# Seven block products in three of eight pairs, and two pairs with adding DMA, in the recurrent-value and gate groups

## The chip, the cores and the metric

The kernel runs on one core of a Trainium2 chip. The metric is the device time of one execution in microseconds. The engines are called by the profile's names: PE is TensorE (PEld its weight loads), DVE is VectorE, ACT is ScalarE, POOL is GpSimd, and SP is the engine that issues most DMAs.

## The reference

The kernel computes one residual block of a streaming encoder on x of 256 tokens and 2048 features, all in float32: an input projection to 7168 columns, eight heads of chunked attention, eight heads of a gated linear recurrence (HGRN2), an output projection, a SwiGLU layer of width 5632 and a last norm.

```python
h = rmsnorm(x, norm1_gain)
proj = h @ w_in          # q_a k_a v_a | q_r f_r i_r g_r, 1024 columns each
attn = rmsnorm(chunk_band_attention(q_a, k_a, v_a, rel_bias), attn_out_gain)
rec = hgrn2_mixer(q_r, f_r, i_r, g_r, lb, grn_norm_gain)   # gated by silu(g_r)
x = x + concat(attn, rec) @ w_out
h2 = rmsnorm(x, norm2_gain)
x = x + (silu(h2 @ w_gate) * (h2 @ w_up)) @ w_down
return rmsnorm(x, final_gain)
```

The change concerns two column blocks of the input projection: i_r, the recurrent values (block "i0" in the code), and g_r, the gates (block "g0"), 1024 columns each.

## The kernel before

**Precision.** Each float32 operand is split in two parts of a shorter format: a high part (ACT copies it with rounding, L89) and a low part (DVE subtracts the high part from the value, L90). A product of two matrices is then three matmuls: high by high, high by low, low by high (L331 to L338, line 336). Weights come from memory in chunks of 1 MB (128 partitions x 2048 columns, that is four blocks of 512 columns) and are split on the core. The input and its split stay in `hx`.

**Groups and pairs.** A `Group` (L315) computes a result of 256 tokens x 1024 columns as four blocks c00, c01, c10, c11 of 128 x 512, each in a bank of accumulators. It walks over the 2048 inputs in eight pairs of 128 rows; a pair needs one chunk of weights. An item of the group's list is a kind and a pair number. Kind "d" (full) makes eight block products, 24 matmuls. Kind "s" makes seven, by a scheme of Strassen's sort: 21 matmuls, some into further banks (m1, m5, m6, m7) that `spread` adds into the output tiles after the last such pair. For it DVE forms differences of weight blocks (`ta`, `tb`, L383 to L387), splits them too, and needs sums of the input blocks, four per pair, that `row_sums` (L290) makes ahead of time. Kind "a" makes eight products like "d", but the low part of the weights comes without DVE: ACT writes the negated high part into a tile (`lower`, L352) and a DMA issued by POOL adds the weights to it from memory (L356). Before the change only the later stages (output projection and gate-up) have "a" items; their chunk lies in a tile of its own, `rawa`, and the adding DMA moves 512 KB.

**The order of the input stage.** Values of attention, then keys and queries of attention, the forget gates f0 and f1 and recurrent queries r0 and r1 of the first four recurrent heads, the recurrent values (one group for all eight heads, `vals`, L874), f2, f3, r2, r3, the gates (`gates`, L885), and then the output projection. `Natural` (L817) is the class of both groups that change. Its items are d0 d1 d2 s6 d3 s7 d4 d5. The row sums for pairs 6 and 7 are in `wsa`, made during attention (`x_sums`, L678); `xs_of` (L814) reads them. In the gates, `wsa` is written anew after item 6, with sums for the output projection (L851).

**Small work between.** What belongs to attention and to the recurrence stands in a list of closures, `queue`. `tick` (L111) runs one entry, or two when more than eight wait, after every chunk of a transposed block (L155). A `Natural` group runs as many entries after an item as its `ticks` say (L848).

**Preparing one item ahead.** `run_groups` (L450) traces an item's matmuls and then the preparation of the next item. When the item after that is an "a", `prepare` traces `begin` (its load) and `lower` first: `lower(0)` ahead of the other splits, and `lower(1)` ahead of them too if the item at hand is an "s", else behind them. The low copies are pinned behind what was traced last on ACT (`keep_in_program_order`, L355); other instructions are ordered when the program is built, by a planner with a list of priorities and estimated durations, and each engine then executes its own list in order.

**Buffers.** Chunks rotate through three places (`wraw`), split halves through four places for high and four for low parts (`wsp`: an "s" takes four of each, a "d" two), differences through one place each (`ta`, `tb` in `dn`). A tile can be written when the last reader of its place is done. SP issues the loads in a fixed order, each behind the one traced before (`dma`, L82).

**Attention's tiles.** For each head `att_scores` (L494) fills `s` (384 columns), `att_probs` (L514) transposes it and fills `pT` (128 columns) and `px` (2 x 256), and `att_values` (L523) multiplies by the values. Three heads are in work at a time: a queue entry runs the values of head n-2, the probabilities of head n-1 and the scores of head n. Each of the three tiles has two places.

Of the kernel before, what the change touches and what calls it, by code (L numbers as in the profile page):

```python
# [8 lines left out]
F32 = mybir.dt.float32  # L9
F32R = mybir.dt.float32r  # L10
I32 = mybir.dt.int32
AF = mybir.ActivationFunctionType
ALU = mybir.AluOpType
# [3 lines left out]
P = 128  # L17
S = 256
# [3 lines left out]
W = 512  # L22
# [23 lines left out]
def hybrid_block(ctx: ExitStack, tc: tile.TileContext, x, xT, w_in, w_out, w_gu, w_down,  # L46
                 bias, gains, lbnd, fgain, out):
    nc = tc.nc
# [33 lines left out]
    def dma(o, i):  # L82
        with ExitStack() as st:
            if prev:
                st.enter_context(tc.issue_after(prev[-1]))
            prev.append(nc.sync.dma_start(o, i).ins)

    def split(hi, lo, src):
        nc.scalar.activation(hi, src, AF.Copy)  # L89
        nc.vector.tensor_tensor(lo, src, hi.bitcast(F32), ALU.subtract)  # L90
# [18 lines left out]
    queue = []  # L109
# [7 lines left out]
    def drain():  # L117
        while queue:
            queue.pop(0)()
# [46 lines left out]
    wsa = tc.tile_pool(name="wsa", bufs=1)  # L166
    own = {"wsa": wsa.__enter__().tile([P, 2, 4, 2, P], F32R, name="wsa")}
    mix = tc.tile_pool(name="mix", bufs=1)
    mixp = mix.__enter__()
    ab = tc.tile_pool(name="ab", bufs=1)  # L170
    abp = ab.__enter__()
# [4 lines left out]
    hx = act_t.tile([P, KD, 2, S], F32R, tag="hx", name="hx")  # L176
# [113 lines left out]
    def row_sums(dst, hi, lo, in_order=False):  # L290
        n = hi.shape[1] // 2
        a = dn.tile([P, 2, 2, S], F32, tag="ta", name="a")[:, 0:n]
        sm = dn.tile([P, 4, 2, P], F32, tag="tb", name="sm")[:, :, 0:n]
        first = nc.vector.tensor_tensor(a, hi.rearrange("p (j k) t -> p j k t", k=2).bitcast(F32),
                                        lo.rearrange("p (j k) t -> p j k t", k=2).bitcast(F32), ALU.add)
        if in_order:
            tc.keep_in_program_order(first)
        a11, a12, a21, a22 = a[:, :, 0, 0:P], a[:, :, 1, 0:P], a[:, :, 0, P:S], a[:, :, 1, P:S]
        nc.vector.tensor_tensor(sm[:, 0], a21, a22, ALU.add)
        nc.vector.tensor_tensor(sm[:, 1], sm[:, 0], a11, ALU.subtract)  # L300
        nc.vector.tensor_tensor(sm[:, 2], a11, a21, ALU.subtract)
        nc.vector.tensor_tensor(sm[:, 3], a12, sm[:, 1], ALU.subtract)
        split(dst[:, 0], dst[:, 1], sm)
# [11 lines left out]
    class Group:  # L315
# [25 lines left out]
            return load_chunk(self.src, self.base + j).rearrange("p (b n) -> p b n", n=W)  # L341

        def begin(self, j):
            raw = own["low"].tile([P, 4, W], F32, name="rawa")
            flat, src = raw.rearrange("p b n -> p (b n)"), self.src[self.base + j]
            if self.src is w_out:
                tc.keep_in_program_order(nc.gpsimd.dma_start(out=flat, in_=src))
            else:
                dma(flat, src)
            self.begun = j, raw, []  # L350

        def lower(self, k):  # L352
            j, raw, low = self.begun
            wl = own["low"].tile([P, 2, W], F32R, tag="low", name="low", bufs=3)
            tc.keep_in_program_order(nc.scalar.activation(wl, raw[:, 2 * k:2 * k + 2], AF.Copy, scale=-1.0))  # L355
            nc.gpsimd.dma_start(out=wl.rearrange("p b n -> p (b n)"),  # L356
                                in_=self.src[self.base + j, :, 2 * k * W:2 * (k + 1) * W], accum_op=ALU.add)
            low.append(wl)

        def prepare_begun(self, j):  # L360
            (_, raw, low), self.begun = self.begun, None
            tiles = []
            for k in range(2):
                wh = wsp.tile([P, 2 * W], F32R, tag="wh", name="wh")
                nc.scalar.activation(wh, raw[:, 2 * k:2 * k + 2].rearrange("p b n -> p (b n)"), AF.Copy)
                tiles.append([(wh[:, i * W:(i + 1) * W], low[k][:, i]) for i in range(2)])
            return [(f"c{t}{h}", self.lhs(2 * j + k, t), tiles[k][h if k == 0 else 1 - h], terms)
                    for terms in ((0, 2), (1,)) for k in range(2) for t in range(NT) for h in range(2)]

# [124 lines left out]
    def att_scores(box, hd, kq, qx, g):  # L494
        h = hd % 4
        sc = paux.tile([P, 384], F32, tag="aux", name="sc")
        nc.tensor.matmul(sc[:, 0:128], lhsT=kq[:, 1, h, :], rhs=kq[:, 0, h, :], start=True, stop=True)  # L497
        kh, kl, qh, ql = kx[:, g, 0, h, :], kx[:, g, 1, h, :], qx[:, 0, h, :], qx[:, 1, h, :]
        nc.tensor.matmul(sc[:, 128:384], lhsT=qh, rhs=kh, start=True, stop=False)
        nc.tensor.matmul(sc[:, 128:384], lhsT=qh, rhs=kl, start=False, stop=False)  # L500
        nc.tensor.matmul(sc[:, 128:384], lhsT=ql, rhs=kh, start=False, stop=True)
        s = box["s"] = abp.tile([P, 384], F32, tag="s", name="s", bufs=2)
        nc.vector.scalar_tensor_tensor(s, sc, ASCALE, G[:, hd, :], ALU.mult, ALU.add)
        nm_ = small.tile([P, 2], F32, tag="nmax", name="nmax")
        sm = small.tile([P, 2], F32, tag="asum", name="asum")
        for t, (a, b) in enumerate(halves):
            nc.vector.tensor_reduce(nm_[:, t:t + 1], s[:, a:b], AX.X, ALU.max, negate=True)
            nc.scalar.activation(s[:, a:b], s[:, a:b], AF.Exp, bias=nm_[:, t:t + 1],
                                 accum_out=sm[:, t:t + 1])
        nc.vector.reciprocal(sm, sm)  # L510
        for t, (a, b) in enumerate(halves):
            nc.vector.tensor_scalar(s[:, a:b], s[:, a:b], sm[:, t:t + 1], None, ALU.mult)

    def att_probs(box):  # L514
        pp = paux.tile([P, 384], F32, tag="aux", name="pp")
        for j in range(3):
            nc.tensor.transpose(pp[:, j * P:(j + 1) * P], box["s"][:, j * P:(j + 1) * P], ident)  # L517
        pT = box["pT"] = abp.tile([P, P], F32, tag="pT", name="pT", bufs=2)
        px = box["px"] = abp.tile([P, 2, S], F32R, tag="px", name="px", bufs=2)
        split(px[:, 0, :], px[:, 1, :], pp[:, 0:256])  # L520
        nc.vector.tensor_copy(pT, pp[:, 256:384])

    def att_values(box, hd, vx, v1, at):  # L523
        h = hd % 4
        hc = slice(h * P, (h + 1) * P)
        px = box["px"]
        po = paux.tile([P, S], F32, tag="aux", name="po")
        nc.tensor.matmul(po, lhsT=vx[:, 0, hc], rhs=px[:, 0, :], start=True, stop=False)
        nc.tensor.matmul(po, lhsT=vx[:, 0, hc], rhs=px[:, 1, :], start=False, stop=False)
        nc.tensor.matmul(po, lhsT=vx[:, 1, hc], rhs=px[:, 0, :], start=False, stop=False)  # L530
        nc.tensor.matmul(po[:, P:S], lhsT=v1[:, hc], rhs=box["pT"], start=False, stop=True)
        nc.scalar.copy(at[:, h, :], po)
# [42 lines left out]
    def attention_end():  # L575
        def flush(n):
            def run():
                att_values(*ago[n - 2])
                if n - 1 < 8:
                    att_probs(ago[n - 1][0])  # L580
            return run
        queue.append(flush(8))
        queue.append(flush(9))
        queue.append(lambda: att_square(1))
        queue.append(att_rstd)
        for g in range(2):
            for i in range(2):
                queue.append(lambda g=g, i=i: att_norm(g, i))
# [87 lines left out]
    vxs = [abp.tile([P, 2, W], F32R, tag="t4", name="vx", bufs=NT4) for _ in range(2)]  # L676
    v1s = [abp.tile([P, W], F32, tag="ht", name="v1", bufs=3) for _ in range(2)]
    def x_sums(j):  # L678
        ks = slice(12 + 2 * j, 14 + 2 * j)
        row_sums(own["wsa"][:, :, :, j:j + 1, :], hx[:, ks, 0, :], hx[:, ks, 1, :])  # L680

    run_groups([Values(0, [("d", j) for j in range(KQ)], w_in, 0, x_pair, None)])
    for g in range(2):
# [15 lines left out]
        if g == 1:  # L699
            queue.insert(0, lambda: att_square(0))  # L700
            dma(lbr.rearrange("p r h -> p (r h)"), lbnd)
            lower_bound()
    attention_end()


    def hgrn_gate(st, g, i):
# [105 lines left out]
        split_scaled(mr[:, 0, ks, tok], mr[:, 1, ks, tok], pt, gg)  # L812

    def xs_of(j, i):  # L814
        return own["wsa"][:, 0, i, j - 6, :], own["wsa"][:, 1, i, j - 6, :]

    class Natural(Group):  # L817
        hold, ready = 1, None

        def __init__(self, nm, func, name, ticks):  # L820
            items = [(c, int(j)) for c, j in zip("dddsdsdd", "01263745")]
            super().__init__(0, items, w_in, chunk_of(nm), x_pair, xs_of)
            self.func, self.ticks = func, ticks
            self.out = [t4([P, NT, W], name) for _ in range(2)]
# [54 lines left out]
    hgrn_front(1)  # L879
    queue.extend(lambda t=t: hgrn_o(sts[1], t) for t in range(NT))  # L880
    x2 = res.tile([P, NT, D], F32, tag="res", name="x2")
    mr = mixp.tile([P, 2, 8, S], F32R, tag="mr", name="mr")
    for t in range(NT):
        dma(x2[:, t, :], x[t])
    gates = Natural("g0", AF.Silu, "gn", {0: 2, 1: 2, 2: 1, 6: 2})  # L885
    for g in range(2):
        sts[g]["gn"] = gates.out[g]

# [59 lines left out]
            Out(1, [(c, int(j)) for c, j in zip("asdsassd", "20316457")], w_out, 8, o_of, wsum_of)]  # L948

    run_groups([gates], wout[0])  # L950
    drain()
    for g in range(2):
        for t in range(NT):
# [274 lines left out]
```

## Time and profile before

| What | Value |
|---|---|
| Median of 3 runs | 1131.99 us (1131.68 to 1132.94) |
| Time of the profiled execution | 1131.58 us |
| Its span, first to last instruction | 1129.9 us |
| Mean granted clock of TensorE | 0.998 |
| Instructions | 14399 |
| Read from memory | 245.92 MB |

The page shows one execution. The lines that matter are the busy time of each engine, the chain of waits that ended last (which engine sets the end), and the groups of instructions with their mean duration. Time of the profile runs from the start of the span. The group of recurrent values lies at about 197 to 240 us, the gates at 291 to 333 us, and the output projection follows.

### The profile page before, as it was taken

The numbers are of one execution on the slowest core, as the hardware profiler recorded it, in microseconds if no ns is written. First come the engines' busy times: TensorE is split into PE (matmuls) and PEld (weight loads), VectorE is DVE, ScalarE is ACT, GpSimd is POOL, SyncE is SP. The second block draws the span as 40 slices with busy tenths as digits, with TensorE's granted clock in tenths as the row PEclk, the third lists the DMA queues.
The fourth block names the chain that finished last, engine by engine and source line by source line (L and its number), as shares of the span: only waits on it lengthen the run. The fifth ranks groups of instructions, "written<-read, shape, count | busy, mean of one in ns | idle before, by whom it ended". The sixth has DMA issues, their size and how long they took to land.

```text
span 1129.9 us, 14399 instructions
## 1 busy us (share of the span) xinstructions
PE 1120.4 (99%) x5344; PEld 936.8 (83%) x5344; DVE 990.0 (88%) x1294; ACT 725.3 (64%) x931; POOL 45.9 (4%) x73
## 2 busy tenths in 40 slices
PE   9999999999999999999999999999999999999997
PEld 7888888888888888888888888888888888888885
DVE  7867778996999998789889989989989999899986
ACT  7555656575966666676676676776766565555563
POOL 0000000000000000000000010010010000000000
PEclk9999999999999999999999999999999999999999
DMA  8665544656355768778788878778788756655652
GB/s 335 211 215 190 182 154 149 224 187 259 140 198 183 227 198 324 223 223 228 264 256 236 267 246 248 266 239 253 254 244 249 286 194 219 223 186 187 222 190 108
DMA packets 40246, 251.05 MB, mean 222 GB/s; under 512 B 4592, under 2 KB 5104, under 8 KB 13424
## 3 DMA queue, kind: packets, MB, share of 16 engines
q1 hardware_dynamic: 32832, 220.51, 53.1%
q0 software_dynamic: 7200, 29.36, 13.4%
q8 instruction: 42, 0.69, 0.2%
q10 hardware_dynamic: 144, 0.26, 0.1%
q14 instruction: 28, 0.23, 0.1%
HBM read 245.92 MB, written 4.19 MB: 221 GB/s over the span
## 4 chain that ended last, share of the span: by engine, by line
PE 98%; DVE 1%; ACT 0%; issue 0%; POOL 0%; ACTq 0%; POOLq 0%
PE c L336 62%; PE m L336 16%; PE acc L151 10%; PE acc L153 5%; PE ptr L281 1%; DVE wl L90 0%; PE wm L181 0%; PE po L792 0%; PE pa L765 0%; PE pp L517 0%; ACT wh L89 0%; PE po L794 0%; PE pc L772 0%; PE pa L780 0%; PE sc L497 0%
## 5 line engine op out<-in xcount | busy, mean ns | idle before, releaser
L90 DVE TENSOR_TENSOR wl<-raw,wh 128x1024 fp32r<-128x1024 f32 (+1 forms) x368 | 403.1, 1112 | 60.8 <-ACT wh L89 58.8
L89 ACT ACTIVATE wh<-raw 128x1024 fp32r<-128x1024 f32 (+1 forms) x368 | 351.8, 971 | 157.5 <-PE c L336 78.6
L336 PE MATMUL c<-wh,h 128*128 128x512 f32 x928 | 274.2, 390 | 0.0
L336 PEld LDWEIGHTS c<-wh,h 128*128 128x128 f32 x928 | 174.1, 188 | 36.6 <-DVE ff L1010 0.3
L151 PE MATMUL acc<-hx,wh 128*128 128x512 f32 x512 | 180.0, 395 | 0.0
L153 PE MATMUL acc<-hx,wl 128*128 128x256 f32 x512 | 143.2, 280 | 0.0
L89 ACT ACTIVATE wh<-ta 128x1024 fp32r<-128x1024 f32 x66 | 70.1, 1062 | 88.5 <-PE c L336 44.2
L336 PE MATMUL c<-wl,h 128*128 128x512 f32 x304 | 119.4, 393 | 0.0
L89 ACT ACTIVATE wh<-tb 128x1024 fp32r<-128x1024 f32 x66 | 70.1, 1062 | 69.0 <-PE c L336 36.3
L151 PEld LDWEIGHTS acc<-hx,wh 128*128 128x128 f32 x512 | 96.0, 188 | 21.4
L336 PE MATMUL c<-wh,hx 128*128 128x512 f32 x336 | 105.8, 393 | 0.0
L90 DVE TENSOR_TENSOR wl<-ta,wh 128x1024 fp32r<-128x1024 f32 x66 | 80.7, 1222 | 19.0 <-ACT wh L89 19.0
L153 PEld LDWEIGHTS acc<-hx,wl 128*128 128x128 f32 x512 | 96.5, 189 | 0.1
L90 DVE TENSOR_TENSOR wl<-tb,wh 128x1024 fp32r<-128x1024 f32 x66 | 80.6, 1221 | 12.2 <-ACT wh L89 9.8
L336 PE MATMUL c<-wh,fh 128*128 128x512 f32 x224 | 87.3, 390 | 0.2 <-DVE ff L1002 0.2
L336 PE MATMUL c<-wh,fl 128*128 128x512 f32 x224 | 87.2, 389 | 0.0
L336 PE MATMUL c<-wl,fh 128*128 128x512 f32 x224 | 87.2, 389 | 0.0
L336 PE MATMUL m<-wh,hs 128*128 128x512 f32 x240 | 81.9, 389 | 0.0
L385 DVE TENSOR_TENSOR ta<-raw 128x1024 f32<-128x1024 f32 x66 | 80.6, 1221 | 0.9
L336 PEld LDWEIGHTS c<-wh,hx 128*128 128x128 f32 x336 | 63.3, 189 | 13.7 <-ACT wh L89 0.5
L336 PEld LDWEIGHTS c<-wl,h 128*128 128x128 f32 x304 | 57.1, 188 | 14.1 <-DVE wl L90 2.5
L336 PE MATMUL c<-wl,hx 128*128 128x512 f32 x168 | 65.2, 393 | 0.0
(354 smaller groups left out, 1735.6 us busy)
## 6 DMA issues: line engine op xcount, KB each, us to landing
raw<-in_w_gu_dram SPq DMA_DIRECT2D x68, 1024.0 KB, 7.0
raw<-in_w_in_dram SPq DMA_DIRECT2D x54, 1024.0 KB, 4.8
raw<-in_w_down_dram SPq DMA_DIRECT2D x44, 1024.0 KB, 4.8
rawa<-in_w_gu_dram SPq DMA_DIRECT2D x20, 1024.0 KB, 6.3
low<-in_w_gu_dram POOLq DMA_DIRECT2D x40, 512.0 KB, 6.9
raw<-in_w_out_dram SPq DMA_DIRECT2D x14, 1024.0 KB, 4.9
x<-in_x_dram SPq DMA_DIRECT2D x2, 1024.0 KB, 7.9
rawa<-in_w_out_dram POOLq DMA_DIRECT2D x2, 1024.0 KB, 7.0
```

The lines of the kernel that those rows point to most:

```text
L89: nc.scalar.activation(hi, src, AF.Copy)
L90: nc.vector.tensor_tensor(lo, src, hi.bitcast(F32), ALU.subtract)
L151: nc.tensor.matmul(ps[m].rearrange("p j t -> p (j t)"), lhsT=wh[:, col], rhs=both, start=kt == 0, stop=False)
L153: nc.tensor.matmul(ps[m][:, 0, :], lhsT=wl[:, col], rhs=rhs[:, kt, 0, :], start=False, stop=kt == KD - 1)
L281: nc.tensor.transpose(pt[:, j, t, :], nat(t)[:, n0 + j * P:n0 + (j + 1) * P], ident)
L336: nc.tensor.matmul(self.bank[n], lhsT=a, rhs=b, start=self.left[n] == self.total[n], stop=self.left[n] == 1)
L385: nc.vector.tensor_tensor(ta, raw[:, 1:3], raw[:, 0:2], ALU.subtract)
```

## The change

- The items of a `Natural` group become d0 a1 s6 d2 s7 s5 a3 d4: three full pairs, three by seven products, two with adding DMA.
- Pair 5 needs row sums. `x_sums(-1)` makes them, as a queue entry behind attention's last, into a new tile `x5`. It takes the place `mr`, which attention's keys `kx` had before and the recurrence's output `mr` has afterwards; `mr` itself is therefore asked for after the gates.
- For this stage an "a" item loads its chunk through the three rotating places (no `rawa`), and makes its low part in four tiles of one block each, with a negating copy of 512 columns and an adding DMA of 256 KB per tile.
- To make room for these, attention's tiles share four places of 512 columns, tag `bx`: `s` and `pT` of a head are one tile, `px` another, and the low tiles use the same four places.
- The gates run three queue entries after item 1 and none after item 2 (before: two and one).

```diff
         def begin(self, j):
+            if self.src is w_in:
+                self.begun = j, self.load(j), []
+                return
...
         def lower(self, k):
             j, raw, low = self.begun
+            if self.src is w_in:
+                low.append([])
+                for b in range(2 * k, 2 * k + 2):
+                    wl = abp.tile([P, W], F32R, tag="bx", name="low", bufs=4)
+                    tc.keep_in_program_order(nc.scalar.activation(wl, raw[:, b], AF.Copy, scale=-1.0))
+                    nc.gpsimd.dma_start(out=wl, in_=self.src[self.base + j, :, b * W:(b + 1) * W], accum_op=ALU.add)
+                    low[k].append(wl)
+                return
...
-            low.append(wl)
+            low.append([wl[:, i] for i in range(2)])
...
-        s = box["s"] = abp.tile([P, 384], F32, tag="s", name="s", bufs=2)
+        bx = box["bx"] = abp.tile([P, W], F32, tag="bx", name="bx", bufs=4)
+        s = box["s"] = bx[:, 0:384]
...
-        pT = box["pT"] = abp.tile([P, P], F32, tag="pT", name="pT", bufs=2)
-        px = box["px"] = abp.tile([P, 2, S], F32R, tag="px", name="px", bufs=2)
+        pT = box["pT"] = box["bx"][:, 384:W]
+        px = box["px"] = abp.tile([P, 2, S], F32R, tag="bx", name="px", bufs=4)
...
     def x_sums(j):
+        if j < 0:
+            own["x5"] = mixp.tile([P, 2, 4, 1, P], F32R, tag="mr", name="x5")
         ks = slice(12 + 2 * j, 14 + 2 * j)
-        row_sums(own["wsa"][:, :, :, j:j + 1, :], hx[:, ks, 0, :], hx[:, ks, 1, :])
+        row_sums(own["wsa"][:, :, :, j:j + 1, :] if j >= 0 else own["x5"], hx[:, ks, 0, :], hx[:, ks, 1, :])
...
     attention_end()
+    queue.append(lambda: x_sums(-1))
...
-            items = [(c, int(j)) for c, j in zip("dddsdsdd", "01263745")]
+            items = [(c, int(j)) for c, j in zip("dasdssad", "01627534")]
...
-    mr = mixp.tile([P, 2, 8, S], F32R, tag="mr", name="mr")
...
-    gates = Natural("g0", AF.Silu, "gn", {0: 2, 1: 2, 2: 1, 6: 2})
+    gates = Natural("g0", AF.Silu, "gn", {0: 2, 1: 3, 6: 2})
...
     run_groups([gates], wout[0])
+    mr = mixp.tile([P, 2, 8, S], F32R, tag="mr", name="mr")
     drain()
```

More of the change, by code (lines that the diff above doesn't have):

```diff
@@ L365, in prepare_begun @@
                 nc.scalar.activation(wh, raw[:, 2 * k:2 * k + 2].rearrange("p b n -> p (b n)"), AF.Copy)
-                tiles.append([(wh[:, i * W:(i + 1) * W], low[k][:, i]) for i in range(2)])
+                tiles.append([(wh[:, i * W:(i + 1) * W], low[k][i]) for i in range(2)])
             return [(f"c{t}{h}", self.lhs(2 * j + k, t), tiles[k][h if k == 0 else 1 - h], terms)
@@ L814, in xs_of @@
     def xs_of(j, i):
+        if j == 5:
+            return own["x5"][:, 0, i, 0, :], own["x5"][:, 1, i, 0, :]
         return own["wsa"][:, 0, i, j - 6, :], own["wsa"][:, 1, i, j - 6, :]
```

## The prediction

> **What bounds the kernel now.** I read the page first (engines, then the chain that ended last), then the chain in order of time, then the busy time by stage for the two groups that the change touches, then their instructions one by one.
>
> ```profile
> span 1129.9 us, 14399 instructions
> PE 1120.4 (99%) x5344; PEld 936.8 (83%) x5344; DVE 990.0 (88%) x1294; ACT 725.3 (64%) x931; POOL 45.9 (4%) x73
> PE 98%; DVE 1%; ACT 0%; issue 0%; POOL 0%; ACTq 0%; POOLq 0%
> ```
>
> The last line is the chain: 98% of the span is TensorE (PE) handing to itself. Matmul ends are modelled, so "99% busy" alone would not do; the starts decide. The chain in order of time (start, length, what, count) shows their spacing in the stretch of values (before 239.6), at the start of the gates, and at the few places where it widens:
>
> ```profile
> 197.57 16.35 PE c L336 x72
> 290.90 16.34 PE c L336 x72
> 319.48 2.29 PE m L336 x9
> 353.90 0.73 PE c L336 x2
> 354.63 0.89 PE m L336 x3
> 368.01 2.14 PE c L336 x8
> ```
>
> 72 matmuls of 512 columns in 16.35 us are 0.227 us each, and the two stretches agree. At that spacing the last four rows would take 2.04, 0.45, 0.68 and 1.82 us, so they hold stalls of 0.25, 0.28, 0.21 and 0.32 us. PE is the bound, with about 1 us of stalls from the gates to the output projection. A change moves the end by the matmuls that it removes plus the stalls that it adds or takes away.
>
> The two groups by stage (PE, PEld, VectorE = DVE, ScalarE = ACT, POOL busy, granted clock, DMA share, GB/s), with the stretch ahead of the first, and below them the rows for the product line L336 alone:
>
> ```profile
> 190.00:200.00 10.00, 10.00 (x56) 8.61 (x55) 9.98 (x18) 7.86 (x12) 0.00 (x0) 1.00 0.47 152
> 197.40:239.60 42.20, 42.20 (x189) 34.92 (x188) 39.20 (x46) 28.52 (x33) 0.00 (x0) 1.00 0.58 202
> 290.70:333.00 42.30, 42.30 (x188) 34.73 (x188) 41.48 (x56) 31.11 (x40) 0.00 (x0) 1.00 0.50 176
> 197.40:239.60 42.20, 42.19 (x186) 34.73 (x186) 1.00 0.58 202
> 290.70:333.00 42.30, 42.30 (x186) 34.69 (x186) 1.00 0.50 176
> ```
>
> In the gates DVE is busy 41.48 of 42.30 us: PE sets the pace, with DVE hardly behind it. ACT has 11 us free there, POOL is idle, DMA is half idle.
>
> **The matmuls.** A full pair costs 8 products of 3 matmuls, 24; a pair by seven products 21. Before, six full and two seven: 6x24 + 2x21 = 186, the count in the rows. After, three full, two with adding DMA (also 24) and three seven: 5x24 + 3x21 = 183. Twice three at 0.227 us: **-1.36 us**. This gain is certain as long as PE is fed. The Trainium skill (TensorE: Matmul & The Clock Gate, Back-to-back issue gap) gives about 131 ns as the sustained spacing at 512 columns and 216 ns for an isolated gap; by the first the term would be -0.79 us, but the rows here show 227 ns, near the second, and the measurement decides.
>
> **DVE and ACT work.** Durations by form in the gates, with the sums of pair 7's size on hx, and the low copies and adding DMAs of the later stages (for those: min/median/max ns; landing in us; the last two rows give size and median landing):
>
> ```profile
> L90 DVE TENSOR_TENSOR wl<-raw,wh 128x1024 fp32r<-128x1024 f32 x14 | 16.9, 1216 | 0.0
> L90 DVE TENSOR_TENSOR wl<-raw,wh 128x512 fp32r<-128x512 f32 x2 | 1.4, 684 | 0.0
> L385 DVE TENSOR_TENSOR ta<-raw 128x1024 f32<-128x1024 f32 x2 | 2.4, 1208 | 0.0
> L387 DVE TENSOR_TENSOR tb<-raw,tb 128x512 f32<-128x512 f32 x2 | 1.4, 688 | 0.0
> L89 ACT ACTIVATE wh<-raw 128x1024 fp32r<-128x1024 f32 x13 | 13.5, 1056 | 4.6 <-PE c L336 2.9 <-DVE wl L90 1.7
> L89 ACT ACTIVATE wh<-raw 128x512 fp32r<-128x512 f32 x2 | 1.3, 626 | 0.3 <-PE m L336 0.3
> L294 DVE TENSOR_TENSOR a<-hx x2: 685/688/692, 36.3 to 39.4; 128x512 f32<-128x512 f32 x2
> L302 DVE TENSOR_TENSOR sm<-a,sm x12: 283/416/424, 39.0 to 1059.2; 128x256 f32<-128x256 f32 x7, 128x128 f32<-128x128 f32 x5
> L356 POOL DMA_DIRECT2D low<-in_w_gu_dram x40: 860/866/892, 458.8 to 861.9; - x40
> DMA to landing us min/median/max: 5.3/7.0/12.7
> low<-in_w_out_dram POOLq DMA_DIRECT2D x4, 512.0 KB, 10.1
> raw<-in_w_in_dram SPq DMA_DIRECT2D x54, 1024.0 KB, 4.8
> ```
>
> On DVE a full pair is 2x1.22 = 2.43 us; a seven-product pair is 0.68 + 1.22 (its blocks), 1.21 + 2x0.69 (differences), 2x1.22 (their splits), 6.92; an adding pair nothing. Per group 6x2.43 + 2x6.92 = 28.4 becomes 3x2.43 + 3x6.92 = 28.1: -0.38. On ACT a full pair is 2.11, a seven-product pair 3.80, an adding pair 2.11 + 4x0.63 = 4.62; per group 20.3 becomes 27.0, +6.7, inside the free 13.7 and 11.2 us. So no engine gets more than it can do; what can cost is the order.
>
> **The row sums of pair 5** (L690, L718): 0.69, four of about 0.28 and a split of 0.68, 2.5 us of DVE once. Counted out, the queue runs them in r1's second chunk: one entry more makes it longer than eight, so it pops two once more and the normalising entries come a chunk earlier. DVE is full there (9.98 of 10), but pair 1's 2.43 us leave just then. Net 0; without that cover at most 2.5 us once.
>
> **Pair 5 behind pair 7, the costly spot.** Two seven-product pairs now follow each other with the low copies of pair 3 between them on ACT: the first is pinned behind what was traced last on ACT, pair 7's fourth split. The same split in the gates before (start, length in us; the first row is r3's evacuation ahead of the gates, the last two low copies of a gate-up group):
>
> ```profile
> 288.84 0.69 ACT L161 COPY tb<-acc 128x256 f32<-128x256 f32 x2
> ...
> 317.28 0.39 PE L336 MATMUL m<-wh,hx 128*128 128x512 f32 x1
> 317.57 1.07 ACT L89 ACTIVATE wh<-tb 128x1024 fp32r<-128x1024 f32 x1 [0.68 <-DVE tb L387]
> 318.62 1.23 DVE L294 TENSOR_TENSOR a<-ma 128x1024 f32<-128x1024 f32 x1
> 319.77 1.22 DVE L90 TENSOR_TENSOR wl<-tb,wh 128x1024 fp32r<-128x1024 f32 x1
> 321.04 0.19 PEld L336 LDWEIGHTS m<-wl,wsa 128*128 128x128 f32 x1 [0.40 <-DVE wl L90]
> ...
> 524.37 2.00 ACT L355 ACTIVATE low<-rawa 128x1024 fp32r<-128x1024 f32 x2
> ```
>
> Pair 7 starts on PE at 317.28. Its fourth tile takes over the place of the pair before, free only then; 15 matmuls later, 3.4 us, it is needed, and ACT 1.07 plus DVE 1.22 leave 1.1 us. One other DVE instruction of 1.23 us (L294) stood between, and PE waited. After the change, counted from pair 7's start: its fourth ACT split ends at 1.4 and four low copies, 0.53 us apart, at 3.5 (two of 1024 columns take 2.00 together in the last row, so each overlaps the one before by 0.1, and 0.63 - 0.1 = 0.53). Pair 5's first split follows until 4.0 and DVE's until 4.7, needed at 4.99 (21 matmuls and one). Its second: ACT 5.0, DVE 6.2, needed at 5.67 (25 matmuls): 0.55 us late. The third and fourth have more room. Bounds per group: nothing, if the low copies find a gap or pair 5's copies are issued ahead of them, to 0.55; I take the middle, **+0.55 us for both groups**.
>
> **What costs nothing.** Pair 1's adding DMAs in the gates: four low copies after r3's evacuation end near 292.0 (289.5 + 4x0.63), and POOL issues at 0.87 us each, the last near 292.8. Its tile is needed 20 matmuls into pair 1, at 290.9 + 24x0.227 + 4.5 = 300.9: 8.1 us for a landing with a median of 7.0 for twice the bytes. The 4 MB more (16 pieces of 256 KB) are small beside DMA half idle. Pair 5's chunk takes the place of the chunk of pair 2, two pairs ahead instead of three, since pair 3's is loaded first. I estimate that pair 2 is split by its own start on PE, 24 + 21 matmuls or 10.2 us before pair 5, against 4.8 us for a load.
>
> Attention's tiles: the place of head n is free after the values of head n, which PE issues ahead of the scores of head n+2; so no new wait. mr takes its place after pair 5's sums are read, and is first written after the gates. The mixed keys move one item earlier, the same three copies.
>
> **The sum.** The profiled execution took 1131.58 us, 1.68 around its span; -1.36 + 0.55 = -0.81 gives 1130.77. Against the median of the three runs, 1131.99 (0.41 above the profiled one): **1131.2**.
>
> **Rivals.**
> *Slower: pair 1's low tiles land late.* The place is the first adding pair of each group, where the copies can't start before the recurrent queries leave PE. For it: the four adding transfers of the output projection took 10.1 us. Against it: those were of 512 KB, and the gate-up ones took 7.0. At 10.1 the last lands 2.0 us late in each group: -1.36 + 4.0 = +2.6, 1134.6. It decides from 8.1 us; at 8.8 it eats the whole gain, at 9.9 it passes 0.2%.
> *Faster: later stalls go as well.* With DVE 0.38 us lighter per group and nothing of pair 3 to split, the 0.25 and the 0.28 + 0.21 + 0.32 us of stalls may vanish: -1.36 - 1.06 = -2.42, 1129.6. Against it: those sit where attention, gates and output projection crowd DVE, and that work stays.
> *No gain in matmuls: DVE is the bound.* Then the end follows DVE: -2x0.38 + 2.5 = +1.74, 1133.7, and the change does not do what it says. For it: 41.48 of 42.30 in the gates; against it: 72 matmuls at 0.227 on both sides, and DVE free for 3 us in the values. The Trainium skill (Perfetto Trace Analysis, Identifying the Most-Contended Engine) wants TensorE judged by its weight loads rather than by matmul occupancy; that is 83% here, below DVE's 88%, and would make this the likeliest case. The even spacing of starts in the trace speaks against it.
>
> **Numbers.** Forecast 0.68 (its own 1130.6 to 1131.7 by the bounds of pair 5's stall), late low tiles 0.14, later stalls gone 0.10, DVE the bound 0.08. The range takes in the second and third rival and the milder half of the first: 1129.6 to 1133.7. A measurement of this kernel can tell about 0.2%, 2.3 us, from no change. Faster by more: most of the second rival, 0.08. Slower by more: the graver part of the first and what I can't see, 0.14. Within: 0.78.
>
> **What would show it.** Right: 183 products in L336's rows for either group; the groups about 0.7 us shorter, less any stall; a small wait of PE at pair 5's second product for DVE or ACT, none at pair 1's low products; the row sums on hx three times, the third ahead of the values; spacing still 0.227. Wrong: PE waiting for a low tile, stalls of over 1 us in a group, or a stretch outside the two groups that grows or shrinks by more than half a microsecond.

## The result and the profile after

The changed kernel takes **1151.05 us** (median of 5 runs, 1148.76 to 1152.89) against 1131.99 us (1131.68 to 1133.19): ratio 1.0167, 95% interval 1.0155 to 1.0178. It is slower by 19 us, where 1131.2 us was forecast. The profiled execution took 1151.12 us, its span 1149.1 us, 19.2 above the span before.

The page of the changed kernel, the lines that answer to those of before:

```profile
span 1149.1 us, 14463 instructions
...
PE 1125.9 (98%) x5338; PEld 938.5 (82%) x5338; DVE 992.9 (86%) x1302; ACT 737.7 (64%) x953; POOL 59.4 (5%) x89
...
q0 software_dynamic: 9504, 33.56, 15.4%
...
PE 91%; DMA 4%; DVE 3%; ACT 1%; issue 0%; SPq 0%; ACTq 0%
PE c L336 58%; PE m L336 15%; PE acc L151 9%; PE acc L153 5%; DMA low<-in_w_in_dram 4%; PE ptr L281 1%; DVE wl L90 1%; ACT wh L89 1%; DMA raw<-in_w_in_dram 0%; PE pa L780 0%; PE po L807 0%; DVE at L565 0%; PE pp L529 0%; DVE ma L90 0%; ACT low L361 0%
...
low<-in_w_in_dram POOLq DMA_DIRECT2D x16, 256.0 KB, 7.2
```

PE has six matmuls fewer, as counted, and still "98% busy": that share hides the loss, because a modelled end stretches over a wait. The chain shows it: PE fell from 98% to 91%, and the new entry is the adding DMA into the low tiles, 4%. The 4%, 46 us of the span, isn't what was lost: the chain follows a transfer back to its issue, also through time in which PE still worked. What PE lost is in the view of its waits (who waited <- for whom: us in total, times, longest):

```profile
PE c L336 <- DMA low<-in_w_in_dram: 13.4, 5, 3.9
PE wm L181 <- POOL ew L182: 1.1, 1, 1.1
```

Five waits, 13.4 us, where before there was none at a transfer. The issues of the adding pieces, on POOL's timeline (start, length, what, count, and in brackets how long POOL had idled, and for whom):

```profile
199.14 2.79 POOL L362 DMA_DIRECT2D low<-in_w_in_dram  x3 [88.03 <-DVE tb L162]
203.94 0.88 POOL L362 DMA_DIRECT2D low<-in_w_in_dram  x1 [2.01 <-ACT qd L772]
228.64 2.60 POOL L362 DMA_DIRECT2D low<-in_w_in_dram  x3 [23.82 <-ACT low L361]
232.52 0.87 POOL L362 DMA_DIRECT2D low<-in_w_in_dram  x1 [1.28 <-ACT wh L89]
300.71 2.62 POOL L362 DMA_DIRECT2D low<-in_w_in_dram  x3 [67.32 <-PE po L809]
304.73 0.87 POOL L362 DMA_DIRECT2D low<-in_w_in_dram  x1 [1.41 <-DMA low<-in_w_in_dram]
330.87 2.62 POOL L362 DMA_DIRECT2D low<-in_w_in_dram  x3 [25.26 <-PE c L336]
335.43 0.86 POOL L362 DMA_DIRECT2D low<-in_w_in_dram  x1 [1.95 <-ACT wh L89]
```

The same picture four times: three pieces go out together, and the fourth 1.3 to 2.0 us after POOL could have issued it. The releasers named differ from row to row and none has to do with this transfer; only one row names an earlier piece of the same kind. By the landings in the trace the first of each three had landed 0.26 to 0.32 us before the fourth went out (at 203.68 the one issued at 199.14). So the fourth looks held until the first has landed; experiment 7 tests it. Now the end of each first adding pair, in the chain in order of time (values, then gates):

```profile
198.27 1.58 ACT low L361 x3
199.84 12.98 DMA low<-in_w_in_dram x2
212.83 0.04 issue
212.87 2.07 PE c L336 x4
214.95 1.28 PE m L336 x3
216.23 2.22 PE c L336 x6
...
300.52 4.21 PE c L336 x19
304.73 9.61 DMA low<-in_w_in_dram
314.34 0.04 issue
314.39 2.07 PE c L336 x4
316.46 1.28 PE m L336 x3
317.74 2.56 PE c L336 x6
```

The fourth piece of the gates, issued at 304.73, lands at 314.34, and PE goes on 0.04 us later. Then the spacing is wrong too: 13 matmuls take 5.57 us in the values and 5.91 in the gates, where 13 x 0.227 is 2.95. The stretches say why (PE, PEld, DVE, ACT, POOL busy, granted clock, DMA share, GB/s):

```profile
207.00:211.00 4.00, 0.96 (x3) 0.49 (x3) 3.49 (x4) 0.77 (x1) 0.00 (x0) 1.00 1.07 270
211.00:215.00 4.00, 2.13 (x5) 1.74 (x6) 0.29 (x1) 0.00 (x0) 0.00 (x0) 0.51 0.47 193
215.00:219.00 4.00, 4.00 (x13) 3.10 (x13) 1.23 (x1) 1.57 (x2) 0.00 (x0) 0.64 0.00 0
309.00:314.00 5.00, 1.51 (x7) 0.93 (x5) 4.59 (x7) 4.97 (x6) 0.00 (x0) 0.95 1.01 251
314.00:319.00 5.00, 4.61 (x11) 3.65 (x12) 2.89 (x4) 1.96 (x3) 0.00 (x0) 0.50 0.26 107
```

Ahead of the end of the wait the DMA engines are busy throughout (a share of 1.07 in the first row and 1.01 in the fourth). Behind it PE runs at about half the clock for some 5 us in the values and 6 in the gates: 2.6 us lost in the values, 3.0 in the gates.

The account: 13.4 us of waits + 5.6 of slow clock - 1.36 of products = 17.6; with 0.8 at pair 5 (below) 18.4 of the 19.2. Nothing lies outside the two groups: by the starts of their products, first to last, the values take 51.6 us instead of 42.0, the gates 51.9 instead of 42.3, 19.2 in sum.

### The profile page after: what moved, and what is told of

The parts are those of the page before. It is cut to its first block, busy times and chain, and to the rows that moved or that the text cites. A ratio compares the mean times of both kernels' runs of the same rounds, so it can differ in the third digit from the quotient of the medians.

```text
span 1149.1 us, 14463 instructions
## 1 busy us (share of the span) xinstructions
PE 1125.9 (98%) x5338; PEld 938.5 (82%) x5338; DVE 992.9 (86%) x1302; ACT 737.7 (64%) x953; POOL 59.4 (5%) x89
## 3 DMA queue, kind: packets, MB, share of 16 engines
q0 software_dynamic: 9504, 33.56, 15.4%
## 4 chain that ended last, share of the span: by engine, by line
PE 91%; DMA 4%; DVE 3%; ACT 1%; issue 0%; SPq 0%; ACTq 0%
PE c L336 58%; PE m L336 15%; PE acc L151 9%; PE acc L153 5%; DMA low<-in_w_in_dram 4%; PE ptr L281 1%; DVE wl L90 1%; ACT wh L89 1%; DMA raw<-in_w_in_dram 0%; PE pa L780 0%; PE po L807 0%; DVE at L565 0%; PE pp L529 0%; DVE ma L90 0%; ACT low L361 0%
## 5 line engine op out<-in xcount | busy, mean ns | idle before, releaser
L90 DVE TENSOR_TENSOR wl<-raw,wh 128x1024 fp32r<-128x1024 f32 (+1 forms) x360 | 393.4, 1109 | 68.8 <-ACT wh L89 66.7
L89 ACT ACTIVATE wh<-raw 128x1024 fp32r<-128x1024 f32 (+1 forms) x360 | 342.3, 967 | 168.0 <-PE c L336 80.8
L90 DVE TENSOR_TENSOR wl<-ta,wh 128x1024 fp32r<-128x1024 f32 x68 | 83.2, 1223 | 19.8 <-ACT wh L89 19.7
L336 PE MATMUL c<-wh,hx 128*128 128x512 f32 x312 | 95.0, 395 | 0.2 <-ACT wh L89 0.2
L90 DVE TENSOR_TENSOR wl<-tb,wh 128x1024 fp32r<-128x1024 f32 x68 | 83.1, 1222 | 10.6 <-ACT wh L89 8.2
L396 DVE TENSOR_TENSOR ta<-raw 128x1024 f32<-128x1024 f32 x68 | 83.1, 1223 | 3.8 <-DMA raw<-in_w_in_dram 1.7
L336 PEld LDWEIGHTS c<-wh,hx 128*128 128x128 f32 x312 | 59.1, 190 | 13.3 <-ACT wh L89 0.9
L367 POOL DMA_DIRECT2D low<-in_w_gu_dram x40 | 34.4, 859 | 393.9 <-ACT low L366 258.8
```

The costliest lines, as they stand in the source:

```text
L336: nc.tensor.matmul(self.bank[n], lhsT=a, rhs=b, start=self.left[n] == self.total[n], stop=self.left[n] == 1)
L367: nc.gpsimd.dma_start(out=wl.rearrange("p b n -> p (b n)"), in_=self.src[self.base + j, :, 2 * k * W:2 * (k + 1) * W], accum_op=ALU.add)
L396: nc.vector.tensor_tensor(ta, raw[:, 1:3], raw[:, 0:2], ALU.subtract)
```

## Experiments

The theory after this look: the low tiles of both adding pairs are late, because their copies are made late, adding pieces are slow, and the fourth is held. The rivals: the new order of items, the shared tiles of attention, or a fuller DVE.

**1. Old items, the rest of the change kept.**

```diff
-            items = [(c, int(j)) for c, j in zip("dasdssad", "01627534")]
+            items = [(c, int(j)) for c, j in zip("dddsdsdd", "01263745")]
```

> The changed kernel with the old list of items (six full pairs, two of seven products): shared attention tiles, row sums of pair 5 (made and not read) and the later place of mr stay. Theory (these parts cost nothing): 1130.5 to 1132 us. Rival (the shared tiles or the 2.5 us of sums on a full VectorE cost time): 1133 us or more.

1131.69 us against 1132.18; ratio 0.9999 (0.9990 to 1.0008). Shared tiles, the sums of pair 5, the later `mr` and the ticks cost nothing. That is as expected, and all of the loss is in the items.

**2. Three seven-product pairs, no adding pair.**

```diff
-            items = [(c, int(j)) for c, j in zip("dasdssad", "01627534")]
+            items = [(c, int(j)) for c, j in zip("ddsdssdd", "01627534")]
```

> Pairs 1 and 3 of both groups are full pairs again, all else as after the change (three seven-product pairs, row sums of pair 5, shared tiles). Late-landing theory: PE waited in the changed kernel for low tiles alone (four stretches, about 20 us of excess between matmul starts with the slow clock behind them), so without adding DMAs nothing of that is left; VectorE gets back 4.9 us per group, which in the full gates may cost 0 to 4 us: 1131 to 1136 us. Rival (the order of seven-product pairs or the shared tiles cost the time): 1148 us or more.

1135.08 us against 1131.05; ratio 1.0035 (1.0022 to 1.0048). The time is in the theory's range, and 15 of the 19 us go with the adding pairs. They also have a use: without them PE waits for splits, as the waits show, and the six products fewer don't pay.

```profile
PE m L336 <- ACT wh L89: 1.4, 2, 0.7
...
PE m L336 <- DVE wl L90: 0.8, 1, 0.8
PE acc L153 <- DVE wl L90: 0.6, 1, 0.6
```

**3. Copy instead of add.**

```diff
-                    nc.gpsimd.dma_start(out=wl, in_=self.src[self.base + j, :, b * W:(b + 1) * W], accum_op=ALU.add)
+                    nc.gpsimd.dma_start(out=wl, in_=self.src[self.base + j, :, b * W:(b + 1) * W])
```

> The changed kernel with the added pass left out of the small pieces of this stage: the sixteen transfers copy the weights into the low tiles in place of adding them, so that the low tiles hold the whole weights (the output is another). Same queue, same ring, same issues. Theory A (a piece is late because adding costs a multiple of moving): a piece lands in 3 to 5 us, the waits at the low tiles fall under 4 us in sum, 1133 to 1138 us. Theory B (it is late by its issue, held by the ring, and by the chunk loads beside it): the fourth piece still lands 8 to 10 us behind its issue, waits 10 us or more, 1145 us or more.

1136.03 us against 1131.84; ratio 1.0036 (1.0023 to 1.0049), as theory A has it. POOL's timeline, and two lines of this kernel's page:

```profile
199.98 2.27 POOL L362 DMA_DIRECT2D low<-in_w_in_dram  x4 [87.97 <-DVE tb L162]
223.03 2.23 POOL L362 DMA_DIRECT2D low<-in_w_in_dram  x4 [20.78 <-ACT low L361]
```
```profile
q0 software_dynamic: 9504, 33.56, 14.5%
...
low<-in_w_in_dram POOLq DMA_DIRECT2D x16, 256.0 KB, 3.8
```

The same bytes in the same number of packets, the negating copies pinned as before: the transfers go out four at a time, none held, and land in 3.8 us at the median instead of 7.2. Of the 13.4 us of waits for low tiles 1.2 are left; waits for splits take their place, 3.3 us. The edit takes away two things at once, the adding and the hold; experiment 8 parts them. In time of the DMA engines: the line of this queue before was

```profile
q0 software_dynamic: 7200, 29.36, 13.4%
```

so the 4.2 MB more cost 15.4% of 1149.1 less 13.4% of 1129.9, 25.6 us of all 16 engines, when added, and by the same subtraction 13.1 us when copied: about twice. The Trainium skill (Collectives: The Full Stack, The bandwidth ceiling: the fold count and why AG ≠ RS ≠ AR) says that a ReduceScatter comes to half the rate of an AllGather, which copies, because its add needs two source reads, by a factor of 1.93 in its measurement. The size agrees in this case, at 1.95 with an uncertainty of about 0.2 from the rounded shares; that two reads are the reason here too is not shown.

**4. All low copies of this stage free to move ahead.**

```diff
-                    tc.keep_in_program_order(nc.scalar.activation(wl, raw[:, b], AF.Copy, scale=-1.0))
+                    nc.scalar.activation(wl, raw[:, b], AF.Copy, scale=-1.0)
```

> The low copies of this stage are no longer pinned behind what was traced last on ScalarE. Pair 1's chunk had landed 9.6 us before its first low copy in the values. Theory: pair 1's pieces are issued 5 to 9 us earlier, the waits at pair 1 (5.2 and 3.9 us, and about 5 us of slow clock behind them) vanish, those at pair 3 (1.9 and 2.7 us) stay or shrink: 1135 to 1139 us. Rival (order of the seven-product pairs): 1148 us or more.

1136.9 us against 1131.05; ratio 1.0056 (1.0039 to 1.0072), as expected. No wait for a low tile is left: the pieces are issued from 185.57, 13.6 us earlier than in the changed kernel. But in the values PE waits for the last split of the seven-product pair 7 (`wl` of `tb`); the wait, and DVE's timeline around it:

```profile
PE m L336 <- DVE wl L90: 2.2, 1, 2.2
```
```profile
216.68 1.23 DVE L90 TENSOR_TENSOR wl<-ta,wh 128x1024 fp32r<-128x1024 f32 x1 [0.24 <-ACT wh L89]
221.44 1.23 DVE L396 TENSOR_TENSOR ta<-raw 128x1024 f32<-128x1024 f32 x1 [3.54 <-DMA raw<-in_w_in_dram]
222.59 1.22 DVE L90 TENSOR_TENSOR wl<-tb,wh 128x1024 fp32r<-128x1024 f32 x1
```

DVE's list has pair 5's difference `ta` ahead of that split, and DVE stood 3.54 us for pair 5's chunk. Its load was issued at 213.96, among the adding pieces of pair 3 (issued from 212.07 to 216.12), and landed at 221.35: 7.4 us, where loads of this size take 4.8 at the median.

What had held the copies in the changed kernel is on ACT's timeline there. In the values pair 1's chunk had landed at 182.02, but the copies are pinned behind the evacuation of the block before (L161):

```profile
197.64 0.63 ACT L161 COPY tb<-acc 128x256 f32<-128x256 f32 x2
198.15 2.21 ACT L361 ACTIVATE low<-raw 128x512 fp32r<-128x512 f32 x4
```

So the chunk lay ready for 16 us. The 9.6 us of the expectation were counted from 188.50, when the next load, that of pair 0, landed: by the semaphores in the trace the low copies read the load that was issued at 177.31.

**5. Only pair 1's low copies free.**

```diff
+                    neg = nc.scalar.activation(wl, raw[:, b], AF.Copy, scale=-1.0)
+                    if j != 1:
+                        tc.keep_in_program_order(neg)
```

> The changed kernel with pair 1's low copies not pinned, and nothing else. Theory (pair 1's lateness comes from the place at which its low copies are made): no wait at pair 1, pair 3 keeps its waits of 1.9 us in the values and 2.7 us in the gates, and no slow clock: 1134 to 1137 us. Rival (the held fourth piece alone makes pair 1 late, wherever the copies stand): pair 1 still waits 3 to 5 us in each group, 1142 us or more.

1138.37 us (1134.14 to 1141.58) against 1131.84; ratio 1.0055 (1.0037 to 1.0074). Pair 1 waits no more, pair 3 does, as expected; the time is 1.4 above the upper end of the theory, which had no slow clock behind a wait of this length; it came. PE's waits for low tiles, and the stretches around the second:

```profile
PE c L336 <- DMA low<-in_w_in_dram: 4.4, 2, 2.3
```
```profile
330.00:333.00 3.00, 0.82 (x5) 0.48 (x3) 3.00 (x7) 2.11 (x3) 0.00 (x0) 1.00 1.02 413
333.00:337.00 4.00, 4.00 (x12) 3.14 (x11) 1.38 (x2) 2.21 (x2) 0.00 (x0) 0.57 0.83 299
```

**6. The values' low parts in two pieces of 512 KB** (a place of the tag `t4` each; the gates unchanged).

```diff
+                if self.func == AF.Copy:
+                    wl = abp.tile([P, 2, W], F32R, tag="t4", name="low2", bufs=NT4)
...
+                    nc.gpsimd.dma_start(out=wl.rearrange("p b n -> p (b n)"),
+                                        in_=self.src[self.base + j, :, 2 * k * W:2 * (k + 1) * W], accum_op=ALU.add)
```

> In the values alone the low part comes in two adding pieces of 512 KB instead of four of 256 KB; the gates keep four. Theory of the held fourth piece: no piece is held in the values, their waits (1.6, 3.6 and 1.9 us) fall to 0 to 3 in sum while the gates keep 3.9 and 2.7: 1142 to 1147 us. Rival (bandwidth alone): the same bytes land at the same time, 1149 to 1152 us.

1146.36 us against 1131.05; ratio 1.0137 (1.0122 to 1.0152). The time is in the theory's range, but not by its terms: the values' waits are 5.0 us in sum, where 0 to 3 were expected. Their pair 3 is in time, pair 1 still waits 2.7 and 2.3 us: issued at 200.51 and 201.43, its pieces land at 209.47 and 213.20. Fewer pieces cure pair 3, and not pair 1, whose copies come late.

**7. The doubled descriptor ring.** Three tries, because the room for it had a price of its own. The ring takes 1 KB more of each partition, and the memory was full; in the first try small tiles gave up their second places (two of these edits are shown).

```diff
-    nc = _bacc.Bacc("TRN2", target_bir_lowering=False, num_devices=1, dynamic_dma_scratch_size=1024)
+    nc = _bacc.Bacc("TRN2", target_bir_lowering=False, num_devices=1, dynamic_dma_scratch_size=2048)
...
-            space = small.tile([P, 3, n], F32, tag=tag, name=tag)
+            space = small.tile([P, 3, n], F32, tag=tag, name=tag, bufs=1)
...
-        junk = ev.tile([P, P], F32, tag="junk", name="junk")
+        junk = ev.tile([P, P], F32, tag="junk", name="junk", bufs=1)
```

> The ring for POOL's descriptors has 2048 instead of 1024 bytes, so that the fourth adding piece need not wait for the first to land (it was issued 0.25 to 0.3 us behind that landing in all four pairs); to make room some small tiles have one place instead of two and some share one, all off the path. Theory of the held fourth piece: it is issued 0.9 us behind the third, lands some 3 us earlier, and the waits of 1.6, 3.6, 1.9, 3.9 and 2.7 us shrink to about 5 in sum, with less slow clock behind them: 1136 to 1143 us. Rival (bandwidth alone: 1 MB added beside two chunk loads takes that long whenever it is issued): the last piece lands when it did, 1148 to 1152 us.

1153.82 us against 1131.05; ratio 1.0202 (1.0187 to 1.0217). The fourth piece was no longer held and the waits fell to 7.8 us, yet the kernel was slower than the changed one: the products of some tiles came 234 ns apart instead of 227, up to the end of the kernel. The second try, with more small tiles in one place, moved them by other amounts:

> The 2048-byte ring once more, with the room made so that every larger tile starts at a multiple of 64 bytes again (with the first ring kernel, products that read tiles behind the shrunk pool were 234 ns apart instead of 227). Theory (held fourth piece, and the tiles' start as the cause of the slower spacing): spacing 227 ns everywhere, waits at pair 1 as in the first ring kernel (5.7 and 2.6 us), none over 0.2 us at pair 3: 1139 to 1144 us. Rival (the ring itself or the slow clock makes the spacing 234): 1150 us or more.

1153.38 us against 1132.18; ratio 1.0187 (1.0173 to 1.0201), with 232 ns: 9 us above the theory and in the rival's range. By this run alone the ring itself could be the cause; experiment 8 decides. The same with pair 1's low copies free (the edit of experiment 5):

> The aligned 2048-byte ring, and pair 1's low copies not pinned on ScalarE (pair 3's stay pinned). Theory: pair 1's pieces are issued 5 to 9 us earlier and its waits go, pair 3's go by the ring; what is left is the removed matmuls, -1.4 us, and 0 to 1.5 us of splits that come late: 1129.5 to 1131.5 us against some 1131.0 before. Rival (adding pieces also hold up the chunk loads beside them, and with them VectorE's splits, as after unpinning all low copies, where PE waited 2.3 us for a split): 1132 to 1135 us.

1141.75 us; ratio 1.0086 (1.0072 to 1.0100), 10 us above the theory, though no wait for a low tile was left. By the starts of the products this kernel is 1.7 us behind the kernel before at 340 us and 9.4 at 1100 us, so most of it arises where the change does nothing.

**8. The kernel before, with a tile of 32 bytes added.**

```diff
+    pad = small.tile([P, 8], F32, tag="pad", name="pad", bufs=1)
+    nc.gpsimd.memset(pad, 0.0)
```

> The kernel before with one more tile of 32 bytes, so that all tiles allocated behind it start 32 bytes later, and one memset of it on POOL; nothing else. Theory of the tiles' start: the products that read tiles behind it are 234 instead of 227 ns apart, some 1000 matmuls of the later stages, 1136 to 1140 us. Rival (the start does not matter): 1131 us.

1140.66 us against 1132.18; ratio 1.0077 (1.0063 to 1.0091): 8.5 us from a tile that nothing reads, a little above the theory's range. The same 120 products of the SwiGLU layer in the chain in order of time, of the kernel before, of this one, and of the second ring kernel:

```profile
898.26 27.23 PE c L336 x120
```
```profile
901.61 27.99 PE c L339 x120
```
```profile
914.72 27.89 PE c L336 x120
```

226.9, 233.3 and 232.4 ns each. The tile moves all pools declared behind `small` by 32 bytes against those ahead of it. Slow are the products with one operand ahead and one behind (weights with `fh`, `fl`, `ma`, `mr`, `wsa`; `low` with the input); weights with `hx`, both ahead, and `low` with `mr`, both behind, keep 227. In the ring kernels `ev` lost 512 bytes and `small` 288 in the first, 384 in the second, so the two halves moved by 800 and 896 bytes against each other. (All moves here are counted from the programs, each tile rounded up to 32 bytes; the trace holds no addresses.) If what counts is that both operands start at the same remainder by 256 bytes, then a shift of 3 x 256 = 768 must cost nothing. That was put to the test, with `small` filled up so that it lost 256, once with the copies pinned as in the change and once with pair 1's free (two tiles of constants became one, which saves the 32 bytes that were wanting):

```diff
+    pad = small.tile([P, 32], F32, tag="pad", name="pad", bufs=1)
+    nc.gpsimd.memset(pad, 0.0)
```

> The changed kernel with the ring doubled and equal remainders, low copies pinned as they are. Theory: what is left of the waits in the doubled ring (1.9 and 4.3 us in the values, 2.8 and 1.0 us in the gates) and the slow clock behind one of them, some 13 us; with products at 227 ns the time is 1142 to 1146 us, 5 to 9 us under the changed kernel. Rival: medians stay at 232 ns and the time at 1153 us.

1144.67 us against 1131.84; ratio 1.0111 (1.0095 to 1.0127): as expected, 8.7 us under the second ring kernel. So the ring itself doesn't slow the products. Against the changed kernel this is the doubled ring's own worth: 6.4 us of the change's loss. Against experiment 3, where nothing is held either, it is 8.6 us more: about what adding costs instead of copying, with the copies pinned. The four pieces go out one behind the other, and pair 1's are late all the same; POOL's timeline and PE's waits:

```profile
199.72 3.66 POOL L366 DMA_DIRECT2D low<-in_w_in_dram  x4 [88.54 <-DVE tb L164]
...
301.57 3.50 POOL L366 DMA_DIRECT2D low<-in_w_in_dram  x4 [67.59 <-PE po L814]
```
```profile
PE c L340 <- DMA low<-in_w_in_dram: 9.1, 4, 3.8
```

> The changed kernel with two mends and their room paid for: the descriptor ring doubled, pair 1's four low copies not pinned, and every pool of tiles shifted by the same bytes, so that the two operands of each product start at the same remainder by 256 bytes, as they do in the kernel before. Theory (the lateness of the low tiles and, in the ring kernels, the unequal remainders are all there is): the medians of the products go back from 232 to 227 ns, which takes some 9 us off the 1141.8 us that the same two mends gave with unequal remainders, no wait stands at a low tile, and the time is 1131.0 to 1132.5 us, level with the kernel before or 0.1% under it. Rival (it is not the remainders, but the place as such, or the doubled ring slows the products): medians stay at 232 ns, 1141 us.

1134.62 us (1133.71 to 1136.25) against 1131.84; ratio 1.0025 (1.0014 to 1.0035). The 120 products take

```profile
900.24 27.22 PE c L340 x120
```

226.8 ns each again, and no wait for a low tile is left. With both mends the change costs 2.8 us instead of 19, but it isn't the 1131.0 to 1132.5 of the theory. In its waits the largest behind the start is

```profile
PE m L340 <- DVE wl L92: 0.7, 1, 0.7
```

at 317.96, the last split of pair 7. It is the place of experiment 4 again, in the gates:

```profile
315.54 1.22 DVE L402 TENSOR_TENSOR ta<-raw 128x1024 f32<-128x1024 f32 x1 [0.24 <-DMA raw<-in_w_in_dram]
316.68 1.22 DVE L92 TENSOR_TENSOR wl<-tb,wh 128x1024 fp32r<-128x1024 f32 x1
```

Pair 5's difference stands ahead of the split and waits for pair 5's chunk, which landed at 315.45, 2.2 us behind pair 7's first product (313.22). The changed kernel has the same order on DVE (`ta` at 329.29, the split at 330.42), but there PE is later, and the chunk landed at 327.61, ahead of pair 7 (328.37). The profiled spans differ by 2.1 us (1132.0 against 1129.9); with the -1.36 that makes 3.5 us to be found. By the starts of the products, 1.8 of them fall between 300 and 340 us, around this wait, 0.5 in the first 20 us, and 1.1 between 80 and 200 us, where attention is worked through. Why that stretch grew stays open; it grew as much in the kernel with the doubled ring and pinned copies, and not in the changed kernel. No version tried beats the kernel before.

## Why the prediction was wrong, point by point

- **Six matmuls, -1.36 us: right.** 5344 became 5338, and wherever PE was fed the spacing stayed at 0.227.
- **Pair 5 behind pair 7, +0.55: right in size.** Around pair 5's first products the starts in the gates are late by 0.64 us together (333.13 to 336.04, ten steps in 2.91 us), in the values by 0.17 (232.35 to 232.97). The sum, 0.8, lies within the bounds, 0 to 1.1. That it comes near the middle is luck in part: the waits at pair 1 had moved everything ahead of it, and the gates alone are above their bound of 0.55.
- **DVE and ACT work, row sums, attention's tiles: right.** Beside pair 5 no product of the two groups waits for a split in the changed kernel, and experiment 1 measured the sums and tiles together at nothing.
- **"Pair 1's adding DMAs in the gates ... 8.1 us for a landing with a median of 7.0 for twice the bytes": the step that failed.** It set the last issue 2.1 us behind the group's start (292.8 less 290.7). It came 4.4 behind it (304.73 less 300.3), 2.3 later. It set the landing at 7.0; it took 9.61, 2.6 more. Of the 2.3 us, 1.4 are the hold of the fourth piece (1.41 in its row), which the prediction didn't have. Together 4.9 us, less the margin of 1.1, is 3.8, and the trace shows a wait of 3.9. "Twice the bytes" was the wrong comfort: the 7.0 us were those of pieces that go out one or two at a time, while here four do within 4 to 5 us, with chunk loads beside them (the load issued at 303.13 took 10.0 us). The row of 10.1 us, of the output projection, was nearer in size and stood in the prediction, as a rival.
- **What wasn't priced at all:** the values, where the copies come later still against their use (waits of 1.6 and 3.6 us at pair 1); pair 3 in both groups (1.9 and 2.7 us); and the slow clock behind a long wait (5.6 us).
- **The rival "pair 1's low tiles land late" was the mechanism**, at 1134.6 us. Its price took one late piece in each group by 2.0 us; there were five waits, and a clock behind them. "The 4 MB more are small beside DMA half idle" is of the same kind: an average over 42 us says nothing of the 10 us behind an issue, in which the DMA share rose to 1.07 and 1.01.
- **"I estimate that pair 2 is split by its own start on PE":** true in the gates of the changed kernel, where pair 5's load was issued at 322.75 and pair 2 began at 322.93. With pair 1's copies free it isn't: in the last kernel of experiment 8 the load was issued at 310.72, 3.1 us behind pair 2's start (307.63). Here and in experiment 4 DVE stood for this chunk, and PE waited 0.7 and 2.2 us behind it.
- **The other rivals** didn't come. DVE did not become the bound: PE waited for splits where the low tiles were in time or left out (experiments 2, 3, 4 and 8), by at most some 3.3 us.

## What to carry to other kernels

A transfer that a bound engine will wait for is priced from its issue to its landing among the transfers issued with it, not from the median of lone ones: count the pieces in flight on its queue, what else loads in these microseconds, and whether it moves or adds. Where copies are pinned, look up what they are pinned behind: here a chunk lay ready for 16 us. And when an experiment makes room by moving tiles, first run the kernel before with that move alone.

## What the runs showed of the hardware

- **Relative start of the two operands.** Float32 products of 512 columns came 231 to 235 ns apart (medians) instead of 227 when the operands' places were moved against each other by 32, 288, 384, 800 or 896 bytes, and 227 when by 0, 256, 512 or 768. (288, 384 and 256 are `low` with the input in the first, the second and the last two ring kernels; 512 are the weights with the input in all four.) A period of 256 bytes fits all nine, one of 128 doesn't.
- **The half clock after a wait.** In the changed kernel the waits of 3.6 and 3.9 us were followed by some 5 and 6 us at half the granted clock, those of 1.9 and 2.7 us by none. The Trainium skill (TensorE: Matmul & The Clock Gate, What's actually happening) says that half rate comes after at least one idle window of about 3.4 us. The gates of the changed kernel agree: PE idles from 310.3, and the clock falls at 313.5. In the values it falls at 211.1, only 1.9 us into the wait of 3.6, with the wait of 1.6 and three products just ahead; and in experiment 5 a wait of 2.3 us was enough (0.57 in the next stretch). The measurement decides: under 3.4 us isn't safe, and the length of the wait alone doesn't settle it. By the traces' records of the granted clock each slow stretch behind such a wait is 3.4, 6.8 or 10.2 us long.
- **Adding transfers.** 256 KB added took 7.2 us to land at the median, copied 3.8, and the time of the DMA engines was about twice. Of four adding pieces in a row the small ring let out three, of four copies all; the doubled ring let out four adding ones. A chunk load issued among adding pieces took 6 to 10 us instead of 4.8 (among copying ones, in experiment 3, up to 7.4).
